# Cutting the first weight chunk into two transfers in a one-core decoder layer

## The chip, the core and the metric

The kernel runs on one NeuronCore of a Trainium2 chip. The work is shared among five engines with their own instruction streams: TensorE (PE in the profile, with its weight loads as PEld), VectorE (DVE), ScalarE (ACT), GpSimd (POOL) and SyncE (SP, which issues nearly all the transfers here). The metric is the device time of one execution in microseconds. The kernel before took 367.78 us, the median of three executions between 367.34 and 368.45 us.

## The reference

The reference is one hybrid decoder layer over 256 positions of width 1024, all in float32:

```python
proj  = x @ w_in                       # -> q | k | v | B | C | h | gate_attn | gate_conv
q, k  = apply_partial_rope(q), apply_partial_rope(k)
y_att = moba_attention(q, k, v) @ w_attn_out     # 256 positions are one block: causal attention
y_cnv = (B * causal_dwconv(C * h)) @ w_conv_out
mix   = (sigmoid(g_att) * y_att + sigmoid(g_cnv) * y_cnv) @ w_o
x     = layer_norm(alpha * x + mix)
u     = causal_dwconv(x @ w_up);  f = (silu(u_gate) * u_val) @ w_down
x     = layer_norm(alpha * x + f)
```

The change touches only the start of the first line, the columns of `proj` that hold q, k and v (512 each).

## The kernel before

**Precision.** Every matrix product is made of three products of TensorE. Each operand is split into a high part (the float32 value copied into the type `fp32r`) and a low part (the value minus its high part). The three passes are high by high (pass 0), high x by low weight (pass 1) and low x by high weight (pass 2). The helper `hl_split` (lines 219 and 220) makes the high part on ScalarE and then the low part on VectorE; the function `split_part` calls it for one slice of a weight.

**Staging.** All weights lie in one packed array in the order of use, in chunks of up to 2048 columns by 128 partitions. `issue_dma` (line 175) fetches a chunk into one of three raw buffers. The first eight chunks each hold 256 columns of the transposed x (one block of 128 of the 1024 input features), then 512 columns of q's weights, 512 of k's and 512 of v's for the same block. A chunk normally is one transfer; the table `PIECES` says at which columns the first two chunks are cut. Before the change, chunk 0 comes in four transfers: x, q's weights, k's weights and v's weights; chunk 1 comes in two: x with q's weights, then k's with v's. A transfer has its own semaphore, and an engine can begin on a piece when that transfer has landed.

**The start of the program.** VectorE sets a small tile of zeros (line 224). TensorE then runs 36 products of that tile with itself (`warm_up`, line 234, 128x128 in bfloat16, whose results are not used), and behind them in its queue come the products of block 0. SyncE issues the transfers of chunks 0 and 1, the small table of constants (line 255) and chunk 2; chunk 3 waits until its raw buffer is free again. For block 0 the splits are written out by hand: VectorE makes the high part of x (line 552), its low part (line 553), the high part of q's weights (line 555) and their low part (line 557); ScalarE and VectorE then split k's weights and v's through `hl_split`. The products are issued by `qkv_passes` (line 546): a product per half of the positions (t = 0, 1) and per pass, each 128x128 by 128x512, six for each of q, k and v of a block. q's six come as passes 0 and 2 of the first half, passes 0 and 2 of the second, then pass 1 of both.

**After block 0.** Blocks 1 to 7 follow in the order q, k, v, and then the rest of the layer, in an order of instructions that is written out by hand for every engine. Nothing behind block 0 is touched by the change.

Of the kernel before, what the change touches and what calls it, by code (L numbers as in the profile page):

```python
# [12 lines left out]
AF = mybir.ActivationFunctionType  # L13
# [3 lines left out]
S = 256  # L17
# [31 lines left out]

CHUNK = 2048  # L50

PIECES = {0: (0, 256, 768, 1280, 1792), 1: (0, 768, 1792)}
OFF_B, OFF_C, OFF_H, OFF_G = 3 * AW, 3 * AW + CW, 3 * AW + 2 * CW, 3 * AW + 3 * CW
TAIL = 8

# [67 lines left out]
def transfers(chunks, units):  # L123

    out, at = [], 0
    for c, us in enumerate(chunks):
        end = units[us[-1]][1] + units[us[-1]][2] * units[us[-1]][3]
        cuts = PIECES.get(c, (0, end))
        assert cuts[-1] == end
# [8 lines left out]
def layer_kernel(ctx: ExitStack, tc: tile.TileContext, x, wpack, cpack, ln1_g, ln1_b, ln2_g, ln2_b, out):  # L138
    nc = tc.nc
# [25 lines left out]
    units = [dict(chunk=c, off=off, shape=(k, n), h=None, l=None) for c, off, k, n, _ in plan_units]  # L165
    raws = []
    XR_CHUNK = 20

    def issue_dma(c):
        while len(raws) <= c and len(raws) < len(chunks):  # L170
            i = len(raws)
            t = wp.tile([P, CHUNK], F32, tag="raw", name=f"raw{i}", bufs=RAW_BUFS)
            raws.append(t)
            for a, b, off in blocks[i]:
                nc.sync.dma_start(t[:, a:b], wpack[off:off + P * (b - a)].rearrange("(p n) -> p n", p=P))
            if i == XR_CHUNK:
                nc.sync.dma_start(xr, x[0].rearrange("(t p) d -> p t d", p=P))
# [21 lines left out]
    def raw_of(u):  # L199
        un = units[u]  # L200
        k, n = un["shape"]
        return raws[un["chunk"]][:, un["off"]:un["off"] + k * n].rearrange("p (k n) -> p k n", k=k)
# [29 lines left out]
    def warm_up(n):  # L232
        for i in range(n):
            nc.tensor.matmul(warm[:, 0:P], zeros, zeros, start=True, stop=True)

    warm_up(36)

    mask = cst.tile([P, 384], F32, name="mask")
    nc.gpsimd.memset(mask, 0.0)
# [20 lines left out]
    xh, xl = xT[:, :, 0], xT[:, :, 1]  # L260
# [275 lines left out]
    def qkv_weights(k, m):  # L536
        ua, ub = (units[U["qkv"] + 3 * k + 1 + e] for e in range(2))
        return (ub["h"][:, 0, :], ub["l"][:, 0, :]) if m == 2 else (ua["h"][:, m, :], ua["l"][:, m, :])
# [3 lines left out]
    def qkv_passes(k, m, ts, ps):  # L542
        wh, wl = qkv_weights(k, m)
        for t in ts:
            for p in ps:
                nc.tensor.matmul(banks[m][t], (xl if p == 2 else xh)[:, k, t * P:(t + 1) * P], wl if p == 1 else wh,  # L546
                                 start=k == 0 and p == 0, stop=k == KT - 1 and p == 2)
# [1 line left out]

    split_start(1)  # L550
    issue_dma(RAW_BUFS - 1)
    nc.vector.tensor_copy(xh[:, 0, :], raws[0][:, 0:S])
    nc.vector.tensor_tensor(xl[:, 0, :], raws[0][:, 0:S], xh[:, 0, :].bitcast(F32), op=ALU.subtract)
    w0, wh0, wl0 = raw_of(1), units[1]["h"], units[1]["l"]
    nc.vector.tensor_copy(wh0[:, 0], w0[:, 0])
    qkv_passes(0, 0, (0, 1), (0, 2))
    nc.vector.tensor_tensor(wl0[:, 0], w0[:, 0], wh0[:, 0].bitcast(F32), op=ALU.subtract)
    qkv_passes(0, 0, (0, 1), (1,))
    split_part(1, 1, 2)
# [489 lines left out]
```

## Time and profile before

| | before |
|---|---|
| median of three executions | 367.78 us (367.34 to 368.45) |
| the profiled execution, its time | 367.38 us |
| the profiled execution, its span | 365.6 us |
| mean granted TensorE clock | 0.994 |
| TensorE busy | 356.8 us, 98% of the span |
| VectorE busy | 296.8 us, 81% |
| ScalarE busy | 222.7 us, 61% |
| bytes read from HBM | 68.24 MB |

The span runs from the first to the last instruction of the profiled execution, and all moments below are counted from its start. Its own time is 1.8 us longer than its span. In the rows of a timeline the first number is the start, the second the duration, then come engine, line and operation; "x4" means that four instructions are merged into one row, and a bracket tells how long the engine had been idle and what released it. Durations of single products on TensorE overlap, since they are pipelined: the distance between two starts is the pace, not the duration.

### The profile page before, as it was taken

Reading aid. Unit: us, or ns where it says so; the run is one execution under the profiler, and the core shown is the slowest. Engines: PE = TensorE matmul, PEld = TensorE weight load, DVE = VectorE, ACT = ScalarE, POOL = GpSimd, SP = SyncE. Lnnn points to the kernel's source line nnn. Section 1 sums busy time; section 2 is a strip of 40 time slices with the busy share of each in tenths; the row PEclk is TensorE's granted clock in tenths of the full one; section 3 lists DMA queues with packets and bytes.
Section 4 is the critical chain, followed back from the end, with each engine's and each line's share of the span. In section 5 each row is a group of like instructions: output and inputs, shape, how many; then the busy total and the mean of one; then the engine's idle time right before and its main releaser. Section 6 shows DMA issues by size and latency. Waiting matters only on the chain.

```text
span 365.6 us, 5224 instructions
## 1 busy us (share of the span) xinstructions
PE 356.8 (98%) x1964; PEld 309.4 (85%) x1964; DVE 296.8 (81%) x510; ACT 222.7 (61%) x380; POOL 13.5 (4%) x34
## 2 busy tenths in 40 slices
PE   8999999999999999999999999999999999999991
PEld 8888888888898888888888888888888888888891
DVE  4885888779986669989769888977768697999884
ACT  4775777576977666653357676664737475767400
POOL 2000000000000003401100000000000000000000
PEclk9999999999999999999999999999999999999997
DMA  8988465335645634588160845447180917663011
GB/s 270 348 296 329 166 230 192 135 117 199 261 163 183 232 115 127 223 331 287 69 230 20 326 136 210 158 189 277 68 329 24 331 57 295 231 229 117 2 57 57
DMA packets 11240, 69.61 MB, mean 190 GB/s; under 512 B 1232, under 2 KB 1616, under 8 KB 4176
## 3 DMA queue, kind: packets, MB, share of 16 engines
q1 hardware_dynamic: 10496, 67.00, 49.6%
q0 software_dynamic: 576, 2.10, 1.7%
q8 instruction: 15, 0.25, 0.3%
q10 hardware_dynamic: 144, 0.20, 0.1%
q14 instruction: 9, 0.07, 0.1%
HBM read 68.24 MB, written 1.05 MB: 190 GB/s over the span
## 4 chain that ended last, share of the span: by engine, by line
PE 98%; DVE 1%; DVEq 0%; issue 0%
PE pb L323 20%; PE pb L330 10%; PE g L323 8%; PE d L305 5%; PE d L306 5%; PE d L307 5%; PE g L330 4%; PE y L323 4%; PE q L546 3%; PE k L546 3%; PE v L546 3%; PE b L323 2%; PE y L330 2%; PE c L323 2%; PE o L305 2%; PE o L307 2%
## 5 line engine op out<-in xcount | busy, mean ns | idle before, releaser
L197 DVE TENSOR_TENSOR wl<-raw,wh 128x1024 fp32r<-128x1024 f32 x99 | 121.1, 1225 | 26.2 <-ACT wh L192 25.8
L192 ACT ACTIVATE wh<-raw 128x1024 fp32r<-128x1024 f32 x99 | 103.6, 1054 | 28.0 <-DMA raw<-in_wpack 28.0
L323 PE MATMUL pb<-x1T,wh 128*128 128x512 f32 x320 | 76.2, 390 | 0.0
L323 PEld LDWEIGHTS pb<-x1T,wh 128*128 128x128 f32 x320 | 59.7, 188 | 12.1
L330 PEld LDWEIGHTS pb<-x1T,wl 128*128 128x128 f32 x320 | 41.0, 191 | 1.6
L330 PE MATMUL pb<-x1T,wl 128*128 128x256 f32 x320 | 41.5, 283 | 0.0
L220 DVE TENSOR_TENSOR wl<-raw,wh 128x1024 fp32r<-128x1024 f32 (+1 forms) x29 | 27.3, 982 | 7.8 <-ACT wh L219 7.5
L323 PE MATMUL g<-xT,wh 128*128 128x512 f32 x128 | 31.7, 394 | 0.0
L305 PE MATMUL d<-wh,f 128*128 128x512 f32 x80 | 31.3, 391 | 0.0
L306 PE MATMUL d<-wl,f 128*128 128x512 f32 x80 | 31.3, 391 | 0.0
L307 PE MATMUL d<-wh,f 128*128 128x512 f32 x80 | 31.1, 389 | 0.0
L219 ACT ACTIVATE wh<-raw 128x1024 fp32r<-128x1024 f32 (+1 forms) x29 | 23.7, 860 | 10.7 <-DMA raw<-in_wpack 6.6
L323 PEld LDWEIGHTS g<-xT,wh 128*128 128x128 f32 x128 | 23.2, 189 | 4.4
L835 DVE SCALAR_TENSOR_TENSOR fc<-fb,consts,fc 128x254 f32<-128x254 f32 x40 | 19.3, 483 | 1.4
L833 DVE SCALAR_TENSOR_TENSOR fc<-fb,consts,fc 128x255 f32<-128x255 f32 x40 | 19.1, 477 | 0.0
L827 ACT ACTIVATE fc<-fb,consts 128x256 f32<-128x256 f32 x40 | 18.0, 497 | 1.7 <-DVE fb L821 1.7
L817 ACT ACTIVATE fb<-pb 128x512 f32<-128x512 f32 x20 | 11.8, 589 | 9.9 <-PE pb L330 9.8
L307 PEld LDWEIGHTS d<-wh,f 128*128 128x128 f32 x80 | 15.0, 188 | 3.2
L305 PEld LDWEIGHTS d<-wh,f 128*128 128x128 f32 x80 | 15.1, 189 | 2.7
L306 PEld LDWEIGHTS d<-wl,f 128*128 128x128 f32 x80 | 15.1, 189 | 2.6
L330 PEld LDWEIGHTS g<-xT,wl 128*128 128x128 f32 x128 | 16.4, 191 | 0.6
L330 PE MATMUL g<-xT,wl 128*128 128x256 f32 x128 | 16.6, 283 | 0.0
(181 smaller groups left out, 576.8 us busy)
## 6 DMA issues: line engine op xcount, KB each, us to landing
raw<-in_wpack SPq DMA_DIRECT2D x55, 1024.0 KB, 5.0
raw<-in_wpack SPq DMA_DIRECT2D x6, 896.0 KB, 5.9
xr<-in_x SPq DMA_DIRECT2D x1, 1024.0 KB, 7.6
ln<-in_ln_g POOLq DMA_DIRECT2D x2, 512.0 KB, 5.5
ln<-in_ln_b POOLq DMA_DIRECT2D x2, 512.0 KB, 6.1
raw<-in_wpack SPq DMA_DIRECT2D x3, 256.0 KB, 3.2
raw<-in_wpack SPq DMA_DIRECT2D x1, 512.0 KB, 5.8
out<-x SPq DMA_DIRECT2D x2, 256.0 KB, 2.0
```

What stands on the lines that cost most here:

```text
L192: nc.scalar.activation(units[u]["h"], raw_of(u), AF.Copy)
L197: nc.vector.tensor_tensor(units[u]["l"], raw_of(u), units[u]["h"].bitcast(F32), op=ALU.subtract)
L219: nc.scalar.activation(h, src, AF.Copy)
L220: (eng or nc.vector).tensor_tensor(l, src, h.bitcast(F32), op=ALU.subtract)
L305: nc.tensor.matmul(o, ah, bh, start=start, stop=False)
L306: nc.tensor.matmul(o, ah, bl, start=False, stop=False)
L307: nc.tensor.matmul(o, al, bh, start=False, stop=stop)
L323: nc.tensor.matmul(bank, un["h"][:, k, n0:n0 + P], b[:, k].rearrange("p a s -> p (a s)"), start=k == 0, stop=False)
L330: nc.tensor.matmul(bank[:, 0:S], un["l"][:, k, n0:n0 + P], b[:, k, 0], start=False, stop=k == nk - 1)
L546: nc.tensor.matmul(banks[m][t], (xl if p == 2 else xh)[:, k, t * P:(t + 1) * P], wl if p == 1 else wh, start=k == 0 and p == 0, stop=k == ...
L833: nc.vector.scalar_tensor_tensor(c[:, 1:S], pb[:, a * S:a * S + S - 1], w_ffn(1, j), c[:, 1:S], op0=ALU.mult, op1=ALU.add)
L835: nc.vector.scalar_tensor_tensor(c[:, 2:S], pb[:, a * S:a * S + S - 2], w_ffn(0, j), c[:, 2:S], op0=ALU.mult, op1=ALU.add)
```

## The change

Three things change, all at the start.

Chunk 0 is now cut like chunk 1: one transfer with x and q's weights (768 columns, 384 KB) and one with k's and v's (1024 columns, 512 KB), instead of four transfers of 128, 256, 256 and 256 KB. The number of warm-up products goes from 36 to 30. In block 0, the high part of x is made by ScalarE instead of VectorE, ahead of ScalarE's split of k's weights, while VectorE makes the high part of q's weights first and the low part of x second; and q's first four products come as pass 0 of both halves, then pass 2 of both halves, so that only the second pair needs the low part of x.

```diff
-PIECES = {0: (0, 256, 768, 1280, 1792), 1: (0, 768, 1792)}
+PIECES = {0: (0, 768, 1792), 1: (0, 768, 1792)}
...
-    warm_up(36)
+    warm_up(30)
...
     split_start(1)
     issue_dma(RAW_BUFS - 1)
-    nc.vector.tensor_copy(xh[:, 0, :], raws[0][:, 0:S])
+    w0, wh0, wl0 = raw_of(1), units[1]["h"], units[1]["l"]
+    nc.scalar.activation(xh[:, 0, :], raws[0][:, 0:S], AF.Copy)
+    nc.vector.tensor_copy(wh0[:, 0], w0[:, 0])
     nc.vector.tensor_tensor(xl[:, 0, :], raws[0][:, 0:S], xh[:, 0, :].bitcast(F32), op=ALU.subtract)
-    w0, wh0, wl0 = raw_of(1), units[1]["h"], units[1]["l"]
-    nc.vector.tensor_copy(wh0[:, 0], w0[:, 0])
-    qkv_passes(0, 0, (0, 1), (0, 2))
+    for p in (0, 2):
+        qkv_passes(0, 0, (0, 1), (p,))
     nc.vector.tensor_tensor(wl0[:, 0], w0[:, 0], wh0[:, 0].bitcast(F32), op=ALU.subtract)
     qkv_passes(0, 0, (0, 1), (1,))
     split_part(1, 1, 2)
```

The packed array is laid out anew to match, with the same bytes in all. Every other instruction keeps its place on its engine.

## The prediction

> **What bounds the kernel now.** I read the page's busy shares and its chain of work first, then the waits of TensorE, then the timeline of the first 10 us.
>
> ```profile
> PE 356.8 (98%) x1964; PEld 309.4 (85%) x1964; DVE 296.8 (81%) x510; ACT 222.7 (61%) x380; POOL 13.5 (4%) x34
> ...
> PE 98%; DVE 1%; DVEq 0%; issue 0%
> ```
>
> ```profile
> PE warm L234 <- DVE zeros L224: 1.0, 1, 1.0
> ```
>
> TensorE is the chain from end to end, and the second fence is the whole answer on whom it waits for: once, for the zeros, before its first instruction. So a microsecond saved elsewhere is worth nothing, and the change can act only on what TensorE does between 0.99 us and the point where the stream is the same again, k's products of block 0. The timeline there, all engines:
>
> ```profile
> 0.74 2.75 SPq L175 DMA_DIRECT2D raw<-in_wpack  x6
> 0.82 0.11 DVE L224 MEMSET zeros<- 128x64 uint32 x1 [0.82 <-PEq L1039]
> 0.99 4.02 PE L234 MATMUL warm<-zeros 128*128 128x128 bf16 x36 [0.99 <-DVE zeros L224]
> ...
> 2.87 0.29 DVE L552 CAST xT<-raw 128x256 fp32r<-128x256 f32 x1 [1.93 <-DMA raw<-in_wpack]
> 3.19 0.43 DVE L553 TENSOR_TENSOR xT<-raw,xT 128x256 fp32r<-128x256 f32 x1
> ...
> 3.85 0.43 DVE L555 CAST wh<-raw 128x512 fp32r<-128x512 f32 x1 [0.23 <-DMA raw<-in_wpack]
> ...
> 4.31 0.69 DVE L557 TENSOR_TENSOR wl<-raw,wh 128x512 fp32r<-128x512 f32 x1
> 4.70 1.37 PEld L546 LDWEIGHTS q<-wh,xT 128*128 128x128 f32 x4
> 4.77 1.73 PE L546 MATMUL q<-wh,xT 128*128 128x512 f32 x4
> 4.89 0.63 ACT L219 ACTIVATE wh<-raw 128x512 fp32r<-128x512 f32 x1 [2.87 <-DMA raw<-in_wpack]
> ...
> 5.68 0.63 ACT L219 ACTIVATE wh<-raw 128x512 fp32r<-128x512 f32 x1 [0.17 <-DMA raw<-in_wpack]
> ...
> 6.34 0.63 PE L546 MATMUL q<-wl,xT 128*128 128x512 f32 x2
> ...
> 6.81 0.62 PE L546 MATMUL k<-wh,xT 128*128 128x512 f32 x2
> 6.91 0.42 ACT L219 ACTIVATE xT<-raw 128x256 fp32r<-128x256 f32 x1 [0.60 <-DMA raw<-in_wpack]
> ...
> 8.19 0.62 PE L546 MATMUL v<-wh,xT 128*128 128x512 f32 x2
> ...
> 9.55 0.39 PE L546 MATMUL q<-wh,xT 128*128 128x512 f32 x1
> ```
>
> q's first operands are ready at 3.85 + 0.43 = 4.28, and its weight load starts only at 4.70, right behind the last warm-up: 0.4 us of real work is held back by warm-ups. The second thing to see is the pace. q's six products take 6.81 - 4.77 = 2.04 us; v's six take 9.55 - 8.19 = 1.36 us. Single starts show where that changes:
>
> ```profile
> 4.77 1.20 PE L546 MATMUL q<-wh,xT 128*128 128x512 f32 x2
> 5.34 0.92 PE L546 MATMUL q<-wh,xT 128*128 128x512 f32 x2
> 5.77 0.73 PE L546 MATMUL q<-wh,xT 128*128 128x512 f32 x2
> 6.11 0.39 PE L546 MATMUL q<-wh,xT 128*128 128x512 f32 x1
> ```
>
> The distances are 0.57, 0.43, 0.34 and then 6.34 - 6.11 = 0.23 us. TensorE runs at about half pace until somewhere between 5.77 and 6.11, some 5 us after its first instruction, although the clock column is 1.00 in these stretches too; before the first recorded change of clock it tells nothing.
>
> **The change, part by part.**
>
> *Six fewer warm-ups.* 36 of them fill 4.77 - 0.99 = 3.78 us, 0.105 us each; 30 end at 0.99 + 3.15 = 4.14. If the operands are there, q starts 0.63 us earlier. That is not 0.63 us of time: up to about 6 us a product takes 0.43 us, and after that 0.23. In 0.63 us of half pace 0.63 / 0.43 = 1.47 products are done, and they would have cost 1.47 x 0.23 = 0.34 us at full pace. Laid out: q's starts become 4.14, 4.71, 5.14, 5.57, 6.00, 6.23 and k starts at 6.46 in place of 6.81. The gain is 0.34 us as long as half pace ends at the same moment, wherever after 4.77 that moment lies.
>
> *The first transfer.* It has 384 KB and must land before q can start, where 128 and then 256 KB did.
>
> ```profile
> raw<-in_wpack SPq DMA_DIRECT2D x3, 256.0 KB, 3.2
> raw<-in_wpack SPq DMA_DIRECT2D x1, 384.0 KB, 4.3
> raw<-in_wpack SPq DMA_DIRECT2D x1, 128.0 KB, 2.1
> ```
>
> ```profile
> 3.00:4.00 1.00, 1.00 (x12) 1.00 (x11) 0.73 (x3) 0.00 (x0) 0.00 (x0) 1.00 1.03 258
> ...
> 6.00:7.00 1.00, 1.00 (x5) 0.82 (x5) 0.89 (x2) 0.40 (x2) 0.00 (x0) 1.00 1.01 352
> 7.00:8.00 1.00, 1.00 (x6) 0.79 (x5) 0.58 (x3) 0.85 (x2) 0.00 (x0) 1.00 1.11 431
> ```
>
> The last column is GB/s. 128 KB were used at 2.87; the 256 KB behind them need 0.61 us at 431 GB/s and 1.02 at 258. So it lands between 2.87 + 0.61 = 3.48 and the 3.85 that the same bytes took before in two transfers. The 384 KB row of 4.3 us (chunk 1, first piece) stood behind 896 KB and is no bound. I take 352 GB/s, the second in which the larger pieces of chunk 1 were moving: 2.87 + 0.75 = 3.62.
>
> *x's high part on ScalarE beside q's weights on VectorE.* ScalarE took 0.42 us for this shape (6.91), VectorE 0.29. From 3.62 both are done by 3.62 + 0.43 = 4.05; with the 0.06 us from zeros (0.82 + 0.11) to the first warm-up (0.99), q can start at 4.11. The warm-ups end at 4.14: no gap, but no margin. With a landing at 3.85 it is 4.34, a gap of 0.20 us at half pace, which takes 0.20 x 0.23 / 0.43 = 0.11 us off the gain. Behind it on VectorE comes x's low part, 4.05 to 4.50; pass 2 wants it at 5.14. q's low weights follow from 4.50 to 5.2, wanted at 6.00. In the landing at 3.85 both shift by 0.23 us and still fit. ScalarE has one more instruction ahead of k's split; it ends a microsecond before k's weights come.
>
> *k and v in one transfer.* The same 896 KB had all landed by 5.68, when v's split began; that is the late bound. From 3.62 on, 512 KB at 352 GB/s give 5.1, and I take that. k's high part would be ready at 5.1 + 0.63 = 5.7, wanted at 6.46. At the late bound it is 6.31 and the low part (0.69 behind it) 7.0 where k's third product wants it at 6.92: a gap of 0.1 to 0.15 us.
>
> *SyncE's queue.* Six issues took 2.75 us, 0.46 each. Two fewer put chunk 1, the constants and chunk 2 on the queue 0.9 us earlier; chunk 1's x, used at 6.91 before, is not later, and block 1's first product is wanted at 9.55 - 0.34 = 9.21. Nothing there had made TensorE wait, and nothing later does: the gain shifts the whole stream.
>
> *Sum.* 0.34 us, or 0.34 - 0.11 - 0.15 = 0.08 at both late bounds. The profiled execution took 367.38, so 367.04 by its own time. The median of the three is 0.40 above that execution; against it the forecast is 367.78 - 0.34 = 367.44, say 367.45. The three differ by 1.11 us, so a change of 0.1% cannot be told from none: 0.3% is 1.1 us.
>
> [...]
>
> **The rivals.**
>
> *TensorE pauses and half pace lasts longer.* If the first transfer lands after 3.65, the warm-ups end before q can start. If such a pause makes the chip count its activity anew, half pace does not end near 6 us. The trace has one figure for how long it looks at TensorE:
>
> ```profile
> 357.80:360.90 3.10, 0.00 (x0) 0.00 (x0) 2.85 (x6) 0.00 (x0) 0.55 (x1) 1.00 0.00 0
> 361.00:365.50 4.50, 0.00 (x0) 0.00 (x0) 1.01 (x2) 0.00 (x0) 0.00 (x0) 0.50 0.31 117
> ```
>
> The seventh figure is the granted clock: it fell to 0.50 some 3.1 us after the last product. Half pace longer by 3.1 us costs 3.1 x (1 - 0.23 / 0.43) = 1.44 us, in all 367.78 - 0.34 + 0.11 + 1.44 = 369.0, slower by 0.33%. For it: there is no margin. Against it: a pause of 0.2 us in 5 us is small, and the 0.57 us between q's first two starts did no harm. [...]
>
> *Half pace ends earlier.* If the moment drifts from execution to execution, the medians drift too. Were TensorE at full pace from 4.14 on, q would take 1.36 us and k start at 5.50: 6.81 - 5.50 = 1.31 us gained, 366.5. For it: 1.11 us between three equal executions, which nothing on the steady chain explains. Against it: it takes the same luck in most executions.
>
> *It does nothing.* Both late bounds together leave 0.08 us: 367.7. The landing of 3.85 and 5.68 in the trace speaks for it, the wider pieces of chunk 1 at 352 to 431 GB/s against it.
>
> **How the numbers follow.** Forecast near 367.45: 0.61. Nothing gained, 367.7: 0.15. Both lie within 0.3%, so same 0.76. Longer half pace, 369.0: 0.12 (0.3 that a pause of over 0.1 us is there, 0.4 that it does such harm). Earlier end, 366.5: 0.12. The range goes from 366.6 to 368.6: it holds the first two cases with about 0.8 us for the drift of medians, and stops short of the two others.
>
> **What would show it.** Right: the first weight load of q at 4.1, k's first product at 6.4 to 6.5 if the 0.23 us pace again begins near 6.0, and the waits of TensorE with the zeros alone. Wrong: a second wait of TensorE, for ScalarE's x or VectorE's weights (first transfer late) or for k's weights (second transfer late); a 0.43 us pace that goes on into k's or v's products; a last product of TensorE that isn't earlier although k started earlier.

## The result and the profile after

The changed kernel took 366.87 us (median of 21 executions, 366.37 to 367.98), the kernel before 367.34 us (median of 21, 366.79 to 368.81). The ratio is 0.9985 with a 95% interval of 0.9978 to 0.9991: 0.55 us faster, between 0.33 and 0.81. That is within 0.3%, as forecast, and a little more than the forecast 0.34. The profiled execution of the changed kernel took 367.11 us, span 365.3. Its page (engines and chain of work):

```profile
PE 357.0 (98%) x1958; PEld 309.0 (85%) x1958; DVE 296.3 (81%) x509; ACT 222.9 (61%) x381; POOL 13.4 (4%) x34
...
PE 98%; DVE 1%; DVEq 0%; issue 0%
```

Nothing has changed in what bounds it. The start, from the timeline:

```profile
0.74 1.79 SPq L175 DMA_DIRECT2D raw<-in_wpack  x4
...
0.99 3.38 PE L234 MATMUL warm<-zeros 128*128 128x128 bf16 x30 [0.99 <-DVE zeros L224]
...
3.73 0.42 ACT L553 ACTIVATE xT<-raw 128x256 fp32r<-128x256 f32 x1 [1.72 <-DMA raw<-in_wpack]
3.74 0.43 DVE L554 CAST wh<-raw 128x512 fp32r<-128x512 f32 x1 [2.80 <-DMA raw<-in_wpack]
4.18 0.42 DVE L555 TENSOR_TENSOR xT<-raw,xT 128x256 fp32r<-128x256 f32 x1
4.28 1.35 PEld L546 LDWEIGHTS q<-wh,xT 128*128 128x128 f32 x4 [0.17 <-ACT xT L553]
4.31 2.05 PE L546 MATMUL q<-wh,xT 128*128 128x512 f32 x4
...
5.88 1.15 ACT L219 ACTIVATE wh<-raw 128x512 fp32r<-128x512 f32 x2 [1.73 <-DMA raw<-in_wpack]
6.16 0.87 PE L546 MATMUL q<-wl,xT 128*128 128x512 f32 x2
...
6.86 0.62 PE L546 MATMUL k<-wh,xT 128*128 128x512 f32 x2
7.29 0.19 PEld L546 LDWEIGHTS k<-wl,xT 128*128 128x128 f32 x1 [0.24 <-DVE wl L220]
```

The steps of the prediction are all there, each a little late: the first transfer is used at 3.73 (forecast 3.62), q's first product starts at 4.31 (4.14) and k's at 6.86. The brackets on the two weight loads are the two waits that the prediction had priced at its late bounds: 0.17 us for x's high part, 0.24 us for k's low part. A weight load that nothing holds starts 0.23 us ahead of its product (7.03 and 7.26 for k's third in the kernel before), so the products lose less: from k's third to its fourth (7.32 to 7.63) it is 0.31 us instead of 0.23, 0.08 lost. And yet k starts no earlier than before (6.81), because in this execution half pace lasted until q's sixth product: that starts at 6.58, 0.42 us behind the fifth, and the first clock record stands at 6.67. TensorE's last product starts at 357.67, 0.15 us later than the 357.52 of before. But the span is 0.23 us shorter. So in this execution the part that was predicted shows no gain as it stands (what half pace hides of it comes below), and 0.38 us were gained behind the last product, where nothing had been predicted. The waits of SyncE's queue from 355 us on show it, before first, then after:

```profile
SPq L1003 <- DVE x L744: 8.9, 1, 8.9
SPq L1045 <- DMA out<-x: 2.4, 1, 2.4
```

```profile
SPq L1004 <- DVE x L745: 8.9, 1, 8.9
SPq L1046 <- DMA out<-x: 2.0, 2, 1.5
```

Behind its last output transfer SyncE waits for transfers once, 2.4 us, in the kernel before; in the changed kernel twice, 2.0 us in all. The raw records of these waits, in us from the start of the last product, tell why:

```
semaphore waited for (in SyncE's order)   before   after
1st                                        6.74     4.37
2nd                                        6.79     4.42
3rd                                        6.86     4.49
4th                                        6.92     4.55
5th                                        6.98     4.62
6th                                        7.04     6.21   <- after: SyncE's output transfer
7th                                        7.10     6.73   <- after: ScalarE's output transfer, the last
8th                                        7.16     6.79
then the drain of SyncE                    7.23     6.86
end of the span                            8.04     7.66
```

At the end of the program SyncE waits for all eight semaphores of its own and ScalarE's transfers, one after the other, about 0.06 us each. In the records of the issues, 73 of SyncE and ScalarE before and 71 after, these eight come in one fixed order, again and again: a transfer does not have a semaphore to itself, as the section on the kernel before has it, but shares it with every eighth transfer. In the kernel before, the last output transfer, which lands at 6.72 (6.71 after), has the first of the eight, so that the seven others come behind it. Two transfers fewer at the start move it to the seventh: five waits are done before the transfer has landed, and one is left behind it. Six waits of 0.063 us are 0.38.

### The profile page after: what moved, and what is told of

Its sections match the earlier page's. It is cut to its first block, busy times and chain, and to the rows that moved or that the text cites. A ratio compares the mean times of both kernels' runs of the same rounds, so it can differ in the third digit from the quotient of the medians.

```text
span 365.3 us, 5209 instructions
## 1 busy us (share of the span) xinstructions
PE 357.0 (98%) x1958; PEld 309.0 (85%) x1958; DVE 296.3 (81%) x509; ACT 222.9 (61%) x381; POOL 13.4 (4%) x34
## 4 chain that ended last, share of the span: by engine, by line
PE 98%; DVE 1%; DVEq 0%; issue 0%
PE pb L323 20%; PE pb L330 10%; PE g L323 8%; PE d L305 5%; PE d L306 5%; PE d L307 5%; PE g L330 4%; PE y L323 4%; PE q L546 3%; PE k L546 3%; PE v L546 3%; PE b L323 2%; PE y L330 2%; PE c L323 2%; PE o L305 2%; PE o L306 2%
## 5 line engine op out<-in xcount | busy, mean ns | idle before, releaser
L848 ACT ACTIVATE f<-ff 128x256 fp32r<-128x256 f32 x22 | 9.1, 414 | 9.7 <-DVE ff L845 9.7
```

## The experiments

All ratios are to the kernel before, run beside them. Two theories stood at first: the six warm-ups are the gain (mine), or the transfers are. Behind each edit stands what was expected before the run.

**30 warm-ups alone.**

```diff
-    warm_up(36)
+    warm_up(30)
```

> The kernel before with 30 warm-up products in place of 36 and nothing else. Theory (fewer warm-ups are the gain, less what TensorE waits): q's operands are ready at 3.85 + 0.43 + 0.06 = 4.34, the warm-ups end at 4.14, so TensorE waits 0.2 us once and the gain is 0.34 - 0.11 = 0.23 us: ratio 0.9994. Rival (the transfers bring the gain): 1.000. Rival (a pause prolongs half pace): slower, ratio 1.003.

Measured: 1.0009 (0.9997 to 1.0021). My 0.9994 lies just outside. The waits of TensorE's weight loads in the first 40 us, behind the warm-ups:

```profile
PEld v L546 <- DVE wl L220: 0.4, 1, 0.4
PEld q L546 <- DVE wl L220: 0.3, 1, 0.3
PEld q L546 <- DVE wh L555: 0.2, 1, 0.2
PEld v L546 <- ACT wh L219: 0.2, 1, 0.2
```

The 0.2 us for q's weights was foreseen. The three others were not: the earlier start runs into v's weights and into block 1, whose first pieces come too late in four transfers. ScalarE began v's split at 6.76 in this profile, not at 5.68, and at 6.44 to 7.21 in the three other profiles with four transfers (below). The 5.68 that I took as the late bound was the earliest of five.

**Transfers and split order alone, 36 warm-ups.** Against the changed kernel:

```diff
-    warm_up(30)
+    warm_up(36)
```

> The changed kernel with 36 warm-ups again: the two transfers and the new order of the splits alone. Theory (fewer warm-ups are the gain): q starts at 4.77 again whatever lands earlier, so ratio 1.000. Rival (the transfers bring the gain, with less traffic at the start): the whole measured gain stays, ratio 0.9985.

Measured: 0.9982 (0.9973 to 0.9991). My theory, 1.000, falls: with the warm-ups back the measured gain is no smaller. (Taken apart below, this run's profile accounts for 0.41 us, a ratio of 0.9989, which lies in the interval.) SyncE's wait for the output was 2.0 us in two pieces here, 2.4 in one piece in the run above.

**Four transfers, with 30 warm-ups and the new split order.** Against the changed kernel:

```diff
-PIECES = {0: (0, 768, 1792), 1: (0, 768, 1792)}
+PIECES = {0: (0, 256, 768, 1280, 1792), 1: (0, 768, 1792)}
```

> The changed kernel, 30 warm-ups and the new order of the splits, but with chunk 0 in four transfers as before. Theory: x's high part is done early, q's weights land at 3.83 and their high part is there at 4.34, so q starts at about 4.34, like the 4.31 of the changed kernel, and the gain is the same within 0.1 us: ratio 0.9985 to 0.999. Rival (the transfers bring the gain): 1.000.

Measured: 1.0001 (0.9988 to 1.0014). Without the two transfers no gain is measured, and my theory falls: q's weights were used at 4.19, not 3.83, and q started at 4.76. The profile again has 2.4 us in one wait at the end, and waits for v's weights (v's split begins at 7.21).

**Two transfers and 30 warm-ups, with the old split order.** The kernel before with the other two edits.

```diff
-PIECES = {0: (0, 256, 768, 1280, 1792), 1: (0, 768, 1792)}
+PIECES = {0: (0, 768, 1792), 1: (0, 768, 1792)}
...
-    warm_up(36)
+    warm_up(30)
```

> The kernel before with two transfers and 30 warm-ups, but with VectorE making x's high part, x's low part and then the high part of q's weights. Theory: the three steps follow one another from 3.73, 0.29 + 0.43 + 0.43 us, so q starts at about 4.98, 0.2 us later than before; TensorE waits 0.8 us: ratio 1.0003 if half pace ends as before. Rival (a pause prolongs half pace): a pause of 0.8 us is four times that of the first run here and shows it, ratio 1.003 or more.

Measured: 1.0012 (0.9998 to 1.0027). TensorE waited once, as expected, for the three steps on VectorE:

```profile
PEld q L546 <- DVE wh L555: 1.0, 1, 1.0
```

q starts at 5.09. In the profile the pause did not prolong half pace, which ended at 4.80, while TensorE still waited. By that profile (below) the ratio should be 0.9999, the lower end of the interval. But the twelve times fall into two groups: five from 366.81 to 367.18 us, the profiled one (366.94) among them, and seven from 368.06 to 369.07, while the 35 of the kernel before beside them reach 368.23. The groups' means are 0.9984 and 1.0032 of the mean of the kernel before, 1.75 us apart. That is near 3.41 x 0.46 = 1.57 us, an estimate of what half pace costs if it lasts 3.41 us longer (the 0.46 is worked out below); about 3.41 us is the step between the distances of the clock records (351.57, 354.99 and 358.40 us, further below). So the pause probably did prolong half pace in most executions, and the rival's 1.003 fits these; no profile of the longer group was taken, so it is not shown.

These four runs do not settle it: the two without the two transfers gain nothing, and of the two with them one measures all of the gain and the other none. I compared the profiles in three numbers: the moment of the trace's first clock record, at which half pace ends (in the kernel before it stands at 5.98, and the products start 0.43 us apart up to 5.77 and 0.23 from 6.11 on); the start of the first product behind block 7, from which to the last product every one of these profiles takes 319.4 us; and the time from the last product's start to the end of the span. By these two paces a microsecond of half pace costs an estimated 1 - 0.23 / 0.43 = 0.46 us, so the second number less 0.46 times the first is the start freed of that drift:

```
                             half pace ends  behind block 7  freed   tail    ratio
before                            5.98           38.11       35.36   8.04    1
after                             6.67           38.27       35.20   7.66    0.9985
30 warm-ups alone                 5.00           37.88       35.58   8.03    1.0009
after, 36 warm-ups                4.69           37.49       35.33   7.66    0.9982
after, four transfers             5.66           38.36       35.76   8.03    1.0001
after, old split order            4.80           37.90       35.69   7.66    1.0012
before, six transfers more        6.34           38.26       35.34   7.66    0.9993
after, two transfers more         5.00           37.43       35.13   8.03    0.9992
before, seven transfers more      5.99           38.12       35.36   7.61    0.9986
after, three cuts                 5.81           37.83       35.16   7.77    0.9976
```

The last four rows belong to the runs that this comparison led to. The first three of these test the end directly: the count of transfers is changed without touching the start.

**Six small transfers more in the kernel before.** They copy 128 x 4 bytes of the constants into a tile that nothing reads.

```diff
+    spare = cst.tile([P, 8], F32, name="spare")
...
+            if 24 <= i < 30:
+                nc.sync.dma_start(spare[:, i - 24:i - 23], cpack[:, i - 24:i - 23])
```

> The kernel before with six more small transfers (128 x 4 bytes each, of the constants into a tile that nothing reads), one behind each of six chunks in the middle. The start is untouched: four transfers, 36 warm-ups. Theory (the gain is at the end: SyncE there waits for eight transfer semaphores one by one, and two transfers fewer move the last output transfer from the first of the eight to the seventh; six more do the same, since 6 = -2 modulo 8): what follows the last product takes 7.66 us instead of 8.04, ratio 0.9990. Rival (the two larger transfers at the start bring the gain): 1.000, or slower by what six transfers cost.

Measured: 0.9993 (0.9980 to 1.0006), and 7.66 us behind the last product. SyncE's waits:

```profile
SPq L1048 <- DMA out<-x: 2.0, 2, 1.6
```

Six transfers were added, and the end became shorter by the 0.38 us expected, with the start as it was (35.34). The time alone could not tell it from no change, since its interval holds 1.000; the profile can.

**Two small transfers more in the changed kernel.** The same lines with `24 <= i < 26`.

> The changed kernel with two of those small transfers more: its start, but the count of transfers of the kernel before. Theory (end): the stretch behind the last product is 8.04 us again and 0.38 of the gain goes; what stays is the start, 0.15 us: ratio 0.9996. Rival (start): the whole gain stays, 0.9985.

Measured: 0.9992 (0.9980 to 1.0004), 8.03 us behind the last product, and the one long wait is back:

```profile
SPq L1049 <- DMA out<-x: 2.4, 1, 2.4
```

The start keeps its gain (35.13).

**Seven small transfers more in the kernel before.** The same lines with `24 <= i < 31`.

> The kernel before with seven more: the last output transfer is then on the eighth semaphore, the last that is waited for. Theory (end): one wait of 0.06 us less than with six, 7.60 us behind the last product, ratio 0.9988; the profile tells it, the times hardly. Rival (start): 1.000.

Measured: 0.9986 (0.9973 to 0.9998), 7.61 us behind the last product; 7.60 was expected. Here the interval leaves 1.000 out: with the start untouched, the end alone makes the program faster.

**Three transfers for chunk 0.**

```diff
-PIECES = {0: (0, 768, 1792), 1: (0, 768, 1792)}
+PIECES = {0: (0, 768, 1280, 1792), 1: (0, 768, 1792)}
```

> The changed kernel with chunk 0 in three transfers: x with q's weights, k's, v's. Theory: k's weights land near 4.9 instead of 5.86, so TensorE no longer waits for k's low part (0.08 us), and the last output transfer moves to the eighth semaphore (0.06 us): 0.14 us faster than the changed kernel, ratio to the kernel before 0.998. Rival (more transfers at the start are what costs): halfway to the kernel before, 0.9992.

Measured: 0.9976 (0.9962 to 0.9989), the lowest of all, with a median of 366.65 us. k's weights were used at 4.48, and the only wait left of TensorE's weight loads behind the warm-ups is that for x:

```profile
PEld q L546 <- ACT xT L553: 0.3, 1, 0.3
```

Its tail was 7.77 us, not the expected 7.60, and SyncE's waits for the output took 2.1 us in that execution, 2.0 in the run with seven more. By the profile's parts 0.47 us of the gain are accounted for, a ratio of 0.9987, which its interval holds. That interval overlaps that of the changed kernel, so that it beats the changed kernel is likely, not shown.

Three more runs tested the prediction's two rivals on half pace.

**One warm-up, 15 warm-ups, 60 warm-ups**, each in the changed kernel; the diff is that of the first.

```diff
-    warm_up(30)
+    warm_up(1)
```

> The changed kernel with a single warm-up product. q starts when its operands are there, at 4.3, as in the changed kernel. Theory (half pace lasts a stretch of steady work, whatever the work): half pace goes on to 8 or 11 us, through q and k and part of v, 3.3 us longer on average at 0.46 us per us: 1.5 us slower than the changed kernel, ratio to the kernel before 1.0026. Rival (half pace ends at a fixed time after the start of the program): as fast as the changed kernel, ratio 0.9985. Rival (warm-ups are useless because the products of q count from the start): also 0.9985.

> The changed kernel with 15 warm-ups: they end at 2.57 and TensorE then waits 1.7 us for q's operands, which come at 4.3. Theory (the pause is counted against the stretch of steady work): half pace ends as if the warm-ups were not there, ratio 1.002 to 1.003. Rival (a pause of under 3 us does no harm): half pace ends near 6 to 7 us as in the changed kernel, ratio 0.9985.

> The changed kernel with 60 warm-ups, 30 more. Theory (a warm-up costs its 128 columns at full pace, 0.23 / 4 = 0.057 us each, since half pace ends at the same moment anyway): 30 x 0.057 = 1.7 us slower than the changed kernel, ratio to the kernel before 0.9985 + 0.0046 = 1.003. Rival (a warm-up costs its own time, 0.105 us): 3.2 us slower, ratio 1.007.

Measured: 1.0014 (1.0003 to 1.0026), 1.0031 (1.0020 to 1.0042) and 1.0019 (1.0008 to 1.0030). The timelines of TensorE with one and with 15:

```profile
4.51 2.05 PE L546 MATMUL q<-wh,xT 128*128 128x512 f32 x4 [3.23 <-DVE wh L554]
6.36 1.05 PE L546 MATMUL q<-wl,xT 128*128 128x512 f32 x2
7.21 1.05 PE L546 MATMUL k<-wh,xT 128*128 128x512 f32 x2
8.06 0.63 PE L546 MATMUL k<-wl,xT 128*128 128x512 f32 x1
```

```profile
0.99 1.78 PE L234 MATMUL warm<-zeros 128*128 128x128 bf16 x15 [0.99 <-DVE zeros L224]
4.40 2.04 PE L546 MATMUL q<-wh,xT 128*128 128x512 f32 x4 [1.62 <-DVE wh L554]
...
8.38 1.05 PE L546 MATMUL k<-wh,xT 128*128 128x512 f32 x2
9.23 0.63 PE L546 MATMUL k<-wl,xT 128*128 128x512 f32 x1
9.65 0.74 PE L546 MATMUL v<-wh,xT 128*128 128x512 f32 x2
```

With one, half pace goes on through q and most of k; the clock record stands at 8.74. (The 8 or 11 us expected were an estimate of mine, which no earlier run shows.) With 15 it goes on to 9.90: the warm-ups ahead of a pause of 1.9 us bought nothing. Freed of that drift their starts are 35.21 and 35.15, like that of the changed kernel. The first was expected at 1.0026 and lies at or under that, the second where it was expected. So half pace does not end at a fixed time, and with a long pause it lasted longer (8.74 and 9.90, against 4.69 to 6.67 with 30 or 36 warm-ups); fixed time and "a pause under 3 us is harmless" both fall. With 60 warm-ups the cost over the changed kernel is 0.0034, or 1.25 us, between 0.6 and 1.9 with the intervals taken together: the 1.7 of the theory fits, the 3.2 of the rival doesn't.

## Why the prediction was right, and where it was not

The range, the sign and "within 0.3%" held. The number held only in part for the reason given, and that the measured 0.55 us lies near the forecast 0.34 is luck: the start gave a half to two thirds of what was forecast for it, and the larger part came from the end, which the prediction had put at nothing. (Of the 0.58 us between the forecast 367.45 and the measured 366.87, 0.44 is the kernel before, 367.34 in 21 executions and 367.78 in the first three.)

*Six fewer warm-ups, 0.34 us.* Mis-sized. Freed of the drift, the start gained 0.16 us in the profile of the changed kernel and 0.23 in that with two transfers more, against three profiles of the old start that agree within 0.02 us. The arithmetic itself held: in the changed kernel with 36 and with 60 warm-ups TensorE waits for no operand of q, k or v, so the 24 more are paid in full. With 60, the first product behind block 7 starts at 39.20; less 0.46 x 5.48 that is 36.68, which is 1.35 us over the 35.33 with 36, or 0.056 us each against the 0.34 / 6 = 0.057 of the sum. (The steady stretch is 319.7 us in the run with 60, 0.3 longer; why is open.) What took the rest are the two late bounds: operands at 4.31 instead of 4.14, and k's low part. The sum with its late bounds gave 0.08; what the profiles show lies between.

*The first transfer, used at 3.62.* Used at 3.73 in the profile of the changed kernel, 0.11 us late, and at 3.80 to 3.95 in the seven others with this transfer. In four of the eight it came after 3.85, the late bound. A rate taken from the stretch of 6 to 7 us was too kind for the first pieces.

*k and v in one transfer, 5.1, at the latest 5.68.* 5.88 in the profile of the changed kernel, 5.07 to 5.65 in the six others with these two transfers. The bound was one execution's good case and no bound. What I missed on the other side is that in four transfers v comes at 5.68 to 7.21. That is why 30 warm-ups alone gain nothing: of the four partial versions none gains more than 0.03 us at the start (35.33 to 35.76, against 35.36), by one profile each; by these it takes all three edits.

*SyncE's queue.* This is the step that was wrong in kind. I followed the two missing issues at the head of the queue and wrote that "nothing later does" wait. I had looked for who waits for SyncE, not for what SyncE waits for at its own end. That wait was in the profile of the kernel before, 2.4 us in one piece behind the last transfer. Its shortening gave 0.38 us, more than the start. Start and end make 0.54 to 0.61 us, and 0.55 was measured.

*Rival: a pause prolongs half pace.* With pauses as short as the changed kernel's there is no sign of it: half pace ended at 5.00 to 6.67 us in the four profiles with pauses of 0.2 to 0.3 us, and at 4.69 to 6.34 us in the four with none. That was the prediction's argument, that 0.2 us in 5 us is small. But longer pauses did harm: one of 1.9 us did in its profile (half pace to 9.90) and its times (1.0031), and one of 1.0 us probably did in seven of twelve executions. From the first clock record to the drop at the end are 354.99 us in eleven of the profiles here, and 351.57 and 358.40 us in the two others (15 and 60 warm-ups): two steps of 3.42 and 3.41 us. What sets the step is not shown.

*Rival: half pace ends earlier.* The drift is real: 4.69 to 6.67 us with 30 or 36 warm-ups, worth 0.9 us between the two ends, about half of the spread of the times (2.0 us in the kernel before, 1.6 in the changed one). That the parts add up to the measured 0.55 suggests that it favoured neither kernel; one profile of each does not show it.

*What would show it.* I named TensorE's own waits as the sign, and that list is silent in the changed kernel: the two waits stand with its weight loads, PEld, which start 0.23 us ahead of the products where nothing holds them.

## What to carry to other kernels

Changing the number of transfers, at the start or in the middle, moved the end of the program here (from 8.04 us behind the last product to 7.66 or 7.61, and back to 8.03): look which of the transfer semaphores the last output has, and whether it is early in the list on which the last engine waits. Compare profiles in parts, the start, the steady stretch and what follows the last product, before believing that a gain comes from where the edit is; here the steady 319.4 us let 0.2 us be seen in a time that spreads by over 1 us. And a bound read from one execution of a transfer is a sample, not a bound.

## What was not expected of the hardware

The length of a pause alone does not tell whether half pace lasts longer. In the run with the old split order TensorE's weight load waited 1.0 us, and half pace ended at 4.80, earlier than the 6.67 of the changed kernel with its wait of 0.17 us for x's high part. With 15 warm-ups it waited 1.9 us, and half pace ended at 9.90; with one it waited 3.4 us, and half pace ended at 8.74. These are single executions, one of each kernel. The two groups of times in the run with the old split order suggest that one and the same pause prolongs half pace in some executions and not in others; what decides it was not tried.

The transfers of the start land unevenly: the piece with v's weights came anywhere from 5.68 to 7.21 us in five profiles with the same four transfers and the same issue times. What holds it up was not settled.
